# Four of 128 expert blocks multiply their tokens as 192 and 64 columns

## The chip, the cores and the metric
One core of a Trainium2 chip runs the whole program in one launch. The metric is the device time of that core in microseconds (us). Two runs of the kernel before took 1375.1 and 1375.38 us, median 1375.24.

## The reference
Two transformer blocks run one after the other on 256 tokens of 1024 features, in float32. The first ends in a retrieval feed-forward layer (PEER): each token chooses, for each of 8 heads, 16 of 16384 single-neuron experts by product keys, and the chosen experts are summed.

```
u_sel = peer_u[expert]
a = jax.nn.gelu(jnp.einsum('bqhkd,bqd->bqhk', u_sel, hb))
v_sel = peer_v[expert]
return jnp.einsum('bqhk,bqhkd->bqd', g * a, v_sel)
```

`g` is the softmax over the 16 chosen scores. The second block (two layers of window attention and gated mixing) follows; the change does not touch it.

## The kernel before
The kernel does not gather experts. It computes the gelu of all 16384 experts for all 256 tokens and multiplies it by a gate that is zero for those not chosen. The experts stand in 128 blocks of 128; a block is a weight tile of 128 partitions x 1024 (8 chunks of 128 features by 128 experts). The tokens `h2` stand transposed, 128 features by 8 chunks by 256 tokens.

Every such product is made in float32 accuracy from three products of rounded operands (type F32R, "round" below): a value is split into a rounded high part and the rest, and high x high, high x rest and rest x high are summed. The weight tile is split when it arrives: ScalarE rounds it into `wh` (line 229), VectorE subtracts to get `wl` (line 232). The tokens are split once, into `h2h` and `h2l`. The profile prints rounded operands of TensorE as f32; which matmuls are rounded is seen from the tiles: those on `wh`/`wl`, `zh`/`zl` and their like. Matmuls on plain F32 tiles, such as those of `proj_block` (line 463: 9 blocks of 8 matmuls, tile `wn` by `hf`) and the token sums (line 286: one column of ones by a 128x128 tile), are not.

The stage that matters here runs `for j in range(128)` over `u_block(j)`. A block loads `u[j]` by the SP queue (3 buffers), splits it (3 buffers each for `wh` and `wl`), and issues 24 matmuls into one PSUM tile of 128x256: for each chunk `k`, lines 246, 247 and 248 of `mm3`. Each matmul has a weight load (LDWEIGHTS) of its own. In the profile line 246 shows as `h2h,wh` (high by high), line 247 as `h2l,wh` and line 248 as `h2h,wl`. ScalarE then writes the gelu of the PSUM tile into `Z[:, j]` (line 927); while gates are built, the tokens whose gates are there already go through `at` and a multiplication on VectorE.

Between the blocks a generator of other steps is drawn on, by a budget of 1.45 per block against a cost that each step yields. First come the rest of the retrieval (top 16 of each head and decoding of the indices, on VectorE nearly alone, lines 822 to 884), then 64 gate steps: one-hot products on VectorE (lines 944 and following), 8 matmuls in f16 (line 951), and a multiplication of `Z` from PSUM. The order of instructions on each engine is the program's order. After the U stage, the V stage multiplies all of `Z` by the V blocks (line 1012), with 24 matmuls of 256 columns for each block, and the second transformer block follows.

The change touches `mm3` (lines 245 to 248), which all these products use, and `u_block`; `mm_block` (line 250) is what the blocks called before. The four changed blocks are j = 2, 34, 66 and 98. In the profiled execution, block 2 runs while VectorE does the retrieval, block 34 in the stretch between the retrieval and the gates, and blocks 66 and 98 among the gate steps.

Of the kernel before, what the change touches and what calls it, by code (L numbers as in the profile page):

```python
# [19 lines left out]
P = 128  # L20
T = 256
D = 1024
NCH = 8
# [141 lines left out]
def build(tc, d, out):  # L165
    nc = tc.nc
    ctx = ExitStack()
    V, S, G, TE = nc.vector, nc.scalar, nc.gpsimd, nc.tensor
# [42 lines left out]
    def nm(s):  # L211
        uid[0] += 1
        return f"{s}_{uid[0]}"
# [5 lines left out]
    def load(src):  # L219
        w = wpool.tile([P, 1024], F32, tag="w", name=nm("w"), bufs=WB)  # L220
        nc.sync.dma_start(w, src)
        return w

    def split(w, hi=S, lo=V, dst=None):
        if dst is None:
            dst = [wpool.tile([P, 1024], F32R, tag=t, name=nm(t), bufs=3) for t in ("wh", "wl")]
        wh, wl = dst
        if hi is S:
            S.activation(wh, w, AF.Copy)  # L229
        else:  # L230
            hi.tensor_copy(wh, w)
        lo.tensor_sub(wl, w, wh.bitcast(F32))  # L232
        return wh, wl
# [9 lines left out]
        return xh, xl  # L243

    def mm3(ps, sh, sl, mh, ml, first, last):
        TE.matmul(ps, sh, mh, start=first, stop=False)  # L246
        TE.matmul(ps, sh, ml, start=False, stop=False)  # L247
        return TE.matmul(ps, sl, mh, start=False, stop=last).ins  # L248

    def mm_block(ps, wh, wl, xh, xl, n=NCH, off=0, xoff=0):  # L250

        for k in range(n):
            sl = slice((off + k) * P, (off + k + 1) * P)
            i = mm3(ps, wh[:, sl], wl[:, sl], xh[:, xoff + k], xl[:, xoff + k], k == 0, k == n - 1)
        return i
# [8 lines left out]
    def mm_rows(src, idx, xh, xl, evac, each=None, sp=split, pre=(), **kw):  # L264

        ps = [psm.tile([P, 512], F32, tag="mm", name=nm("psr")) for _ in range(2)]
        for g in range(4):
            wh, wl = sp(pre[g] if g < len(pre) else load(src[idx + g]), **kw)
            for q in range(2):
                k = 2 * g + q  # L270
                for t in range(2):
                    ts_ = slice(t * P, (t + 1) * P)
                    mm3(ps[t], xh[:, k, ts_], xl[:, k, ts_],
                        wh[:, q * 512:(q + 1) * 512], wl[:, q * 512:(q + 1) * 512], k == 0, k == 7)
            if each:
                each()
        for t in range(2):
            evac(t, ps[t])

    def psum_mm():  # L280
        return psm.tile([P, 512], F32, tag="mm", name=nm("psmm"))
# [54 lines left out]
    def aux():  # L336
        return psa.tile([P, 512], F32, tag="aux", name=nm("aux"))
# [18 lines left out]
    for i in range(2):  # L356
        sl = slice(512 * i, 512 * i + 512)
        ps = aux()
# [20 lines left out]
    for i in range(4):  # L379
        ps = psum_mm()  # L380
# [21 lines left out]
    for k in range(NCH):  # L402
# [8 lines left out]
        sh = mod1[:, k, 1:2]  # L411
# [154 lines left out]
    for g in range(4):  # L566
        for q in range(2):
            k = 2 * g + q
# [16 lines left out]
    last = [None]  # L585
# [55 lines left out]
    for hp in range(4):  # L641
        ps = aux()
# [84 lines left out]
    for s in range(EARLY):  # L727
        w = nload()
        ps = psum_mm()
# [21 lines left out]
    h2h = pu.tile([P, NCH, T], F32R, name="h2h")  # L751
    h2l = pu.tile([P, NCH, T], F32R, name="h2l")
# [164 lines left out]
    last_mm, last_act = [None], [None]  # L917
    done = [0]

    def u_block(j):  # L920

        wh, wl = split(load(d["u"][j]))
        ps = psum_mm()
        last_mm[0] = mm_block(ps[:, :T], wh, wl, h2h, h2l)
        nd = done[0]
        if nd < T:
            last_act[0] = S.activation(Z[:, j, nd:], ps[:, nd:T], AF.Gelu_apprx_tanh).ins
        if nd:
            at = pr.tile([P, T], F32, tag="at", name=nm("at"), bufs=2)
            S.activation(at[:, :nd], ps[:, :nd], AF.Gelu_apprx_tanh)  # L930
            V.tensor_mul(Z[:, j, :nd], Z[:, j, :nd], at[:, :nd])
# [48 lines left out]
    for j in range(NJ):  # L980
        u_block(j)
        ju[0] = j + 1
        budget += STEP
        while budget > 0:
            c = next(todo, None)
            if c is None:
                break
            budget -= c
# [59 lines left out]
    def next2():  # L1048
        w = load(d["w2"][w2i[0]])
        w2i[0] += 1  # L1050
        return w

    def split2(w, dst=None):
        return split(w, dst=dst)
# [9 lines left out]
    def rows_tile(t, xh, xl, slabs, late_x=False):  # L1064

        ps = psum_mm()
        ts_ = slice(t * P, (t + 1) * P)
        for c in range(2):
            passes = [((xh, 0), (xh, 1)), ((xl, 0),)] if late_x else [((xh, 0), (xl, 0)), ((xh, 1),)]
            for r, ops in enumerate(passes):  # L1070
                for k in range(4 * c, 4 * c + 4):
                    sl = slice((k % 2) * 512, (k % 2) * 512 + 512)
                    for i, (x, part) in enumerate(ops):
                        last_mm[0] = TE.matmul(ps, x[:, k, ts_], slabs[k // 2][part][:, sl],  # L1074
                                               start=k == 0 and r == 0 and i == 0, stop=k == NCH - 1 and r == 1).ins
        return ps
# [15 lines left out]
    for l in range(2):  # L1092
        xh, xl = xh4, xl4
        if l == 0:
            first = []
# [30 lines left out]
        else:  # L1126
            ps = rows_tile(0, xh, xl, ahead, True)
# [11 lines left out]
        ps = aux()  # L1139
# [109 lines left out]
        for g in range(4):  # L1249
            ps = aux()  # L1250
# [8 lines left out]
        for b in range(4):  # L1259
            ps = aux()  # L1260
# [17 lines left out]
        mh = p4.tile([P, NCH, T], F32R, tag="mh", name=f"mh{l}")  # L1278
        ml = p4.tile([P, NCH, T], F32R, tag="ml", name=f"ml{l}")
        for n in range(NCH):  # L1280
            wh, wl = split2(next2())
# [16 lines left out]
        for t in range(2):  # L1298
            for hf in range(2):
                sl = slice(hf * 512, (hf + 1) * 512)  # L1300
# [14 lines left out]
        last = []  # L1315
# [48 lines left out]
```

## Time and profile before

| | |
|---|---|
| median of the runs | 1375.24 us |
| the profiled execution | 1375.99 us |
| its span, from the first to the last instruction | 1373.5 us |
| TensorE matmuls, busy | 1349.5 us (98%), 10472 |
| TensorE weight loads, busy | 1291.5 us (94%), 10472 |
| VectorE, busy | 1016.0 us (74%) |
| ScalarE, busy | 627.9 us (46%) |
| mean granted TensorE clock | 0.995 |

A matmul's duration in the profile runs from its start to the end of its drain, so consecutive matmuls overlap: what a matmul costs a full engine is the time from one start to the next. A row "x6" merges six instructions of the same form in a row: its duration runs from the first start to the last end. A weight load's row (PEld) overlaps the matmul before it.

### The profile page before, as it was taken

Reading aid. Unit: us, or ns where it says so; the run is one execution under the profiler, and the core shown is the slowest. Engines: PE = TensorE matmul, PEld = TensorE weight load, DVE = VectorE, ACT = ScalarE, POOL = GpSimd, SP = SyncE. Lnnn points to the kernel's source line nnn. Section 1 sums busy time; section 2 is a strip of 40 time slices with the busy share of each in tenths; the row PEclk is TensorE's granted clock in tenths of the full one; section 3 lists DMA queues with packets and bytes.
Section 4 is the critical chain, followed back from the end, with each engine's and each line's share of the span. In section 5 each row is a group of like instructions: output and inputs, shape, how many; then the busy total and the mean of one; then the engine's idle time right before and its main releaser. Section 6 shows DMA issues by size and latency. Waiting matters only on the chain.

```text
span 1373.5 us, 26275 instructions
## 1 busy us (share of the span) xinstructions
PE 1349.5 (98%) x10472; PEld 1291.5 (94%) x10472; DVE 1016.0 (74%) x2091; ACT 627.9 (46%) x1098; POOL 20.5 (1%) x35
## 2 busy tenths in 40 slices
PE   8999999999999999999999999999999999999997
PEld 6868899999999999999999999999999999799996
DVE  7898499974777777875777767666676867858676
ACT  5534255544544444444333333333345665356642
POOL 1000000000000000000000000000010000000000
PEclk9999999999999999999999999999999999999999
DMA  9886245566544454445666666656576466544663
GB/s 375 305 318 234 85 153 158 169 195 182 161 138 144 134 154 138 139 140 177 214 208 201 213 200 200 185 184 184 181 222 199 139 226 188 183 147 146 197 193 117
DMA packets 72554, 255.01 MB, mean 186 GB/s; under 512 B 8305, under 2 KB 10481, under 8 KB 72178
## 3 DMA queue, kind: packets, MB, share of 16 engines
q1 hardware_dynamic: 72434, 253.36, 57.7%
q8 instruction: 82, 1.34, 0.4%
q14 instruction: 38, 0.31, 0.1%
HBM read 252.28 MB, written 1.05 MB: 184 GB/s over the span
## 4 chain that ended last, share of the span: by engine, by line
PE 84%; DVE 11%; ACT 1%; DMA 1%; issue 1%; DVEq 0%; POOL 0%; SPq 0%; POOLq 0%; ACTq 0%
PE vacc L1012 26%; PE psmm L246 13%; PE psmm L248 13%; PE psmm L247 13%; PE aux L951 4%; DVE wl L232 3%; PE psmm L677 2%; PE psmm L1074 2%; PE aux L443 2%; PE psmm L463 1%; DMA w<-w 1%; PE iqp L443 1%; DVE Z L826 1%; DVE Z L824 1%; DVE Z L823 1%
## 5 line engine op out<-in xcount | busy, mean ns | idle before, releaser
L229 ACT ACTIVATE wh<-w 128x1024 fp32r<-128x1024 f32 x373 | 394.5, 1060 | 502.9 <-PE vacc L1012 206.8
L232 DVE TENSOR_TENSOR wl<-w,wh 128x1024 fp32r<-128x1024 f32 x373 | 455.2, 1221 | 157.3 <-ACT wh L229 155.0
L246 PE MATMUL psmm<-h2h,wh 128*128 128x256 f32 x1136 | 328.7, 289 | 0.0
L248 PE MATMUL psmm<-h2h,wl 128*128 128x256 f32 x1136 | 323.2, 285 | 3.6 <-DVE wl L232 3.5
L247 PE MATMUL psmm<-h2l,wh 128*128 128x256 f32 x1136 | 322.0, 283 | 0.0
L1012 PE MATMUL vacc<-zh,wh 128*128 128x256 f32 x1024 | 290.0, 284 | 0.4 <-DVE zh L241 0.4
L1012 PE MATMUL vacc<-zl,wh 128*128 128x256 f32 x1024 | 290.2, 284 | 0.0
L1012 PE MATMUL vacc<-zh,wl 128*128 128x256 f32 x1024 | 290.2, 284 | 0.0
L248 PEld LDWEIGHTS psmm<-h2h,wl 128*128 128x128 f32 x1136 | 217.5, 192 | 5.8 <-DVE wl L232 5.7
L246 PEld LDWEIGHTS psmm<-h2h,wh 128*128 128x128 f32 x1136 | 218.7, 193 | 0.1
L247 PEld LDWEIGHTS psmm<-h2l,wh 128*128 128x128 f32 x1136 | 218.1, 192 | 0.1
L1012 PEld LDWEIGHTS vacc<-zh,wh 128*128 128x128 f32 x1024 | 196.6, 192 | 0.5 <-issue 0.5
L1012 PEld LDWEIGHTS vacc<-zl,wh 128*128 128x128 f32 x1024 | 196.9, 192 | 0.0
L1012 PEld LDWEIGHTS vacc<-zh,wl 128*128 128x128 f32 x1024 | 196.9, 192 | 0.0
L246 PE MATMUL psmm<-xh,wh 128*128 128x256 f32 x544 | 154.4, 284 | 0.0
L248 PE MATMUL psmm<-xh,wl 128*128 128x256 f32 x544 | 152.2, 280 | 0.0
L247 PE MATMUL psmm<-xl,wh 128*128 128x256 f32 x544 | 151.9, 279 | 0.0
L246 PEld LDWEIGHTS psmm<-xh,wh 128*128 128x128 f32 x544 | 102.2, 188 | 0.9 <-ACT yh L1272 0.3
L248 PEld LDWEIGHTS psmm<-xh,wl 128*128 128x128 f32 x544 | 102.3, 188 | 0.7 <-DVE mx L1174 0.7
L247 PEld LDWEIGHTS psmm<-xl,wh 128*128 128x128 f32 x544 | 102.1, 188 | 0.1
L241 DVE CAST zh<-Z 128x256 fp32r<-128x256 f32 x128 | 37.4, 293 | 69.7 <-PE vacc L1012 69.3
L944 DVE TENSOR_TENSOR oh<-iohr,ij 128x1024 f16<-128x1024 f16 x64 | 44.2, 692 | 54.9 <-PE aux L951 54.9
(390 smaller groups left out, 1780.8 us busy)
## 6 DMA issues: line engine op xcount, KB each, us to landing
w<-u SPq DMA_DIRECT2D x128, 512.0 KB, 3.5
w<-v SPq DMA_DIRECT2D x128, 512.0 KB, 3.6
w<-w SPq DMA_DIRECT2D x122, 512.0 KB, 3.6
ada<-ada SPq DMA_DIRECT2D x40, 512.0 KB, 6.1
wn<-w SPq DMA_DIRECT2D x23, 512.0 KB, 5.4
w<-wa SPq DMA_DIRECT2D x8, 512.0 KB, 7.1
wb<-wb SPq DMA_DIRECT2D x8, 512.0 KB, 4.7
w<-ada SPq DMA_DIRECT2D x8, 512.0 KB, 3.5
```

The lines of the kernel that those rows point to most:

```text
L229: S.activation(wh, w, AF.Copy)
L232: lo.tensor_sub(wl, w, wh.bitcast(F32))
L241: hi.tensor_copy(xh, src)
L246: TE.matmul(ps, sh, mh, start=first, stop=False)
L247: TE.matmul(ps, sh, ml, start=False, stop=False)
L248: return TE.matmul(ps, sl, mh, start=False, stop=last).ins
L443: TE.matmul(ps, st, mv, start=first, stop=e and part == 1, skip_group_check=True)
L677: TE.matmul(ps, w[:, sl], y[:, k], start=half == 0 and q == 0 and k == 0, stop=half == 1 and k == 3, skip_group_check=True)
L944: V.tensor_tensor(oh, bc(iohr.unsqueeze(1), [P, 2, P, 4]), bc(ij16[:, :, k:k + 4].unsqueeze(2), [P, 2, P, 4]), ALU.is_equal)
L951: TE.matmul(o, oh[:, 0, :, q], ow[:, r, :, q], start=r == 0, stop=r == 1)
L1012: TE.matmul(acc[k // 2][:, k % 2], a[:, sl], b, start=(f and i == 0), stop=(l and i == 2), skip_group_check=True)
L1074: last_mm[0] = TE.matmul(ps, x[:, k, ts_], slabs[k // 2][part][:, sl], start=k == 0 and r == 0 and i == 0, stop=k == NCH - 1 and r == 1).ins
```

## The change
`u_block` takes its 256 tokens in two pieces for j = 2, 34, 66 and 98. For each chunk it first issues the three products for tokens 0 to 191, then the three for tokens 192 to 255, into the two parts of the same PSUM tile; only the very first matmul of the block carries the start flag. So such a block has 24 matmuls of 192 columns and 24 of 64, where it had 24 of 256. In `mm3` a flag is set that leaves out a check when the program is built.

```
 def mm3(ps, sh, sl, mh, ml, first, last):
-    TE.matmul(ps, sh, mh, start=first, stop=False)
-    TE.matmul(ps, sh, ml, start=False, stop=False)
-    return TE.matmul(ps, sl, mh, start=False, stop=last).ins
+    TE.matmul(ps, sh, mh, start=first, stop=False, skip_group_check=True)
+    TE.matmul(ps, sh, ml, start=False, stop=False, skip_group_check=True)
+    return TE.matmul(ps, sl, mh, start=False, stop=last, skip_group_check=True).ins
...
-    last_mm[0] = mm_block(ps[:, :T], wh, wl, h2h, h2l)
+    if j % 32 == 2:
+        for k in range(NCH):
+            sl = slice(k * P, (k + 1) * P)
+            for ts_ in (slice(0, 192), slice(192, T)):
+                last_mm[0] = mm3(ps[:, ts_], wh[:, sl], wl[:, sl], h2h[:, k, ts_], h2l[:, k, ts_], k == 0 and ts_.start == 0, k == NCH - 1)
+    else:
+        last_mm[0] = mm_block(ps[:, :T], wh, wl, h2h, h2l)
```

## Rows read from the trace of the kernel before
**Rows 1.** The page: busy us, share of the span and instructions of each engine.
```profile
PE 1349.5 (98%) x10472; PEld 1291.5 (94%) x10472; DVE 1016.0 (74%) x2091; ACT 627.9 (46%) x1098; POOL 20.5 (1%) x35
```
**Rows 2.** Chain of waits by time, 220 to 300 us: start, us, what.
```profile
224.76 1.12 DVE wl L232
...
279.96 1.15 DVE wl L232
281.15 0.38 PE psmm L248
```
**Rows 3.** Busy time by stretch: length; PE, PEld, DVE, ACT, POOL busy; PEclk; DMA.
```profile
225.50:229.00 3.50, 3.42 (x28) 3.10 (x26) 3.50 (x23) 1.33 (x2) 0.00 (x0) 1.00 0.43 150
...
284.00:360.00 76.00, 76.00 (x637) 76.00 (x636) 41.03 (x48) 38.44 (x57) 0.00 (x0) 1.00 0.62 189
360.00:626.00 266.00, 266.00 (x2226) 262.50 (x2224) 202.63 (x333) 119.71 (x278) 0.00 (x0) 1.00 0.46 143
...
656.00:1018.00 362.00, 361.64 (x3015) 361.46 (x3014) 253.62 (x403) 134.95 (x129) 0.13 (x1) 1.00 0.63 196
```
**Rows 4.** TensorE in order of time, first matmuls of blocks 34 and 35.
```profile
324.20 0.28 PE L246 MATMUL psmm<-h2h,wh 128*128 128x256 f32 x1
...
327.08 0.28 PE L246 MATMUL psmm<-h2h,wh 128*128 128x256 f32 x1
```
**Rows 5.** TensorE in order of time, a gate step and the start of block 66.
```profile
435.00 1.11 PE L951 MATMUL aux<-ow,oh 128*128 128x128 f16 x8
435.86 0.38 PE L246 MATMUL psmm<-h2h,wh 128*128 128x256 f32 x1
```
**Rows 6.** TensorE's waits from 284 us on: total us, times, longest us.
```profile
PE aux L1085 <- DVE xr L1335: 2.5, 1, 2.5
```
**Rows 7.** VectorE's waits from 284 to 660 us.
```profile
DVE oh L944 <- PE aux L951: 54.9, 62, 1.5
```
**Rows 8.** TensorE in order of time near the end, rounded, 512 columns.
```profile
1363.02 0.40 PE L1074 MATMUL psmm<-wlast_yh,ml 128*128 128x512 f32 x1
...
1364.42 0.40 PE L1074 MATMUL psmm<-wlast_yl,ml 128*128 128x512 f32 x1
```
**Rows 9.** Weight loads in order of time, token sums of one column.
```profile
119.90 0.97 PEld L286 LDWEIGHTS aux<-ones,nsq 128*128 128x128 f32 x8 [0.38 <-ACT nsq L654]
```
**Rows 10.** Line 463, unrounded: in order of time, then as a group.
```profile
84.26 1.46 PE L463 MATMUL psmm<-hf,wn 128*128 128x256 f32 x6
...
L463 PE MATMUL psmm<-hf,wn 128*128 128x256 f32 x144 | 33.9, 383 | 0.0
```
**Rows 11.** TensorE in order of time, second and third matmuls of blocks 3 to 6.
```profile
228.80 0.28 PE L247 MATMUL psmm<-h2l,wh 128*128 128x256 f32 x1
230.32 0.39 PE L248 MATMUL psmm<-h2h,wl 128*128 128x256 f32 x1 [1.24 <-DVE wl L232]
...
233.18 0.28 PE L247 MATMUL psmm<-h2l,wh 128*128 128x256 f32 x1
233.82 0.39 PE L248 MATMUL psmm<-h2h,wl 128*128 128x256 f32 x1 [0.36 <-DVE wl L232]
...
236.67 0.28 PE L247 MATMUL psmm<-h2l,wh 128*128 128x256 f32 x1
237.20 0.39 PE L248 MATMUL psmm<-h2h,wl 128*128 128x256 f32 x1 [0.24 <-DVE wl L232]
...
240.05 0.28 PE L247 MATMUL psmm<-h2l,wh 128*128 128x256 f32 x1
240.73 0.39 PE L248 MATMUL psmm<-h2h,wl 128*128 128x256 f32 x1 [0.40 <-DVE wl L232]
```
**Rows 12.** ScalarE in order of time: gelu of block 2, rounding for block 5.
```profile
233.30 0.36 ACT L927 ACTIVATE Z<-psmm 128x256 f32<-128x256 f32 x1
233.56 1.05 ACT L229 ACTIVATE wh<-w 128x1024 fp32r<-128x1024 f32 x1
```
**Rows 13.** VectorE in order of time, subtraction for block 5.
```profile
235.94 1.20 DVE L232 TENSOR_TENSOR wl<-w,wh 128x1024 fp32r<-128x1024 f32 x1
```

## The prediction
> **What bounds the kernel now.** I begin with the page's busy shares: TensorE is busy for 98% of the span, VectorE for 74% [rows 1]. So a longer U block should cost its whole extra length wherever TensorE leads, and the question is which of the four changed blocks (U2, U34, U66, U98) lie where it does not. The chain in order of time answers it for U2. From 224.76 us, where this part of it begins, to 281.15 us, where the chain goes over to a U matmul, its pieces are VectorE's [rows 2]: the retrieval, and between its steps the subtractions that give `wl`. U3's second matmul starts at 228.80 us [rows 11], so U2 is the 3 us before that, inside this stretch.
>
> The busy time by stretches says the same. From 225.5 to 229 us VectorE is busy for 3.50 of 3.50 us, from 284 to 360 us TensorE for 76.00 of 76.00, from 360 to 626 us for 266.00 of 266.00, and in the V stage for 361.64 of 362.00 [rows 3]. Since a matmul's row contains its drain, "busy" alone does not prove a dense engine; starts do. U34's first matmul starts at 324.20 us and U35's at 327.08 us, so 24 matmuls take 2.88 us, **0.120 us each** [rows 4]. In the gate stage, block and gate matmuls follow each other too: the eight of a gate start at 435.00 us and U66 at 435.86 us, 0.86 us [rows 5]. After 284 us TensorE has four waits to the end of the program, the longest 2.5 us for a transpose between the two layers [rows 6]; that one stands after work which starts later by the same amount, so it gives nothing back. VectorE in turn waits for the gate matmuls 62 times, 54.9 us in all [rows 7], so it has room and will not become the bound when TensorE is later. U34, U66 and U98 therefore pass their extra time to the end.
>
> **The change, part by part.** Nothing is moved and no tile, load, queue entry or semaphore wait is added: DMA, ScalarE and VectorE issue what they issued. The flag on the matmul helper changes a check at build time and costs nothing, there being no instruction for it. Each changed block gives up 24 matmuls of 256 columns and gets 24 of 192 and 24 of 64, each with its own weight load. That is 96 more matmuls and 96 more loads over the four blocks. The columns to stream stay 256 per chunk and product, so what is new is the price of the second instruction.
>
> No matmul of rounded (F32R) operands narrower than 256 columns is in the trace, so I bound the pair.
> - From below, by streaming alone. At 512 columns seven starts span 1363.02 to 1364.42 us, six steps of 0.233 us [rows 8]; with 0.120 at 256 [rows 4] that is a line of 0.007 + 0.00044 x columns. It gives 0.092 us for 192 and 0.035 us for 64, together 0.127 against 0.120: +0.17 us for a block.
> - From the rows with few columns. The one-column matmuls of the token sums have nothing to stream, and yet their eight weight loads of 128x128 take 0.97 us with the last one's 0.19 us included: (0.97 - 0.19) / 7 = **0.111 us each** [rows 9]. This is the time from one weight load to the next when the matmul hides none of it.
> - From above, by the price of unrounded fp32. Six records of 256 columns take 1.46 us, the last with its 0.38: 0.216 us each [rows 10], and the group counts 144 records for 9 blocks of 8 matmuls, two for each matmul. So 256 columns cost 0.432 us, 192 would cost 0.324, and 64 between 0.111 (one load) and 0.222 (two).
>
> I take the middle row. The 192-column matmul is nearest to the 256-column one, 0.120 us, for its stream of 0.092 is shorter than a weight load and cannot set the pace. The 64-column one is nearest to the one-column row, 0.111 us. A block then takes 24 x 0.231 = 5.54 us instead of 2.88, **+2.66 us**.
>
> Three blocks pay it in full: 3 x 2.66 = +8.0 us. U2's +2.66 us falls into waits for `wl`. U3's second and third matmul start at 228.80 and 230.32 us, where 0.12 would do: 1.40 us of room. U4 has 233.18 to 233.82 (0.52), U5 236.67 to 237.20 (0.41), U6 240.05 to 240.73 (0.56) [rows 11]. That is 2.89 us, so the delay is 1.26 us after U3, 0.74 after U4, 0.33 after U5 and nothing after U6, if VectorE is not late itself. What VectorE could wait for is ScalarE's rounding for U5, queued on ScalarE behind U2's gelu. That gelu starts at 233.30 us [rows 12], and U2 would end by 231.5 us, so nothing waits. If this cover failed, the sum would be 4 x 2.66 = 10.6 us.
>
> The profiled execution took 1375.99 us, of which 1373.5 is its span; with +8.0 it would take 1384.0. The median of the runs lies 0.75 lower, at 1375.24, which gives **1383.2 us**, +0.6%.
>
> **Rivals.**
> 1. *The weight load hides, and only columns count* (not slower). Place: all four blocks; price: the line above, +0.17 us each, three of them on the path: 1375.7 us. It decides if the next weights load twice as fast when the current matmul is short. Against it stands the 0.111 us of rows with one column [rows 9]; for it, only that those are unrounded operands. Chance 0.07. The Trainium skill, in "TensorE: Matmul & The Clock Gate", section "Back-to-back issue gap", gives a warm isolated matmul N/2.4 + 2.5 ns: 82.5 and 29.2 ns here, less than the one of 256, and so a result some 0.6 us under the time before. By that section's sustained figure, 131 ns for 512 columns with its load, this trace disagrees, with 233 ns.
> 2. *Narrow rounded matmuls lose their single pass* (slower). Place: the array; price: the unrounded rate, 24 x (0.324 + 0.111 - 0.120) = +7.6 us for a block, up to 24 x (0.324 + 0.222 - 0.120) = +10.2. It decides if the single pass is only to be had from 256 columns up. For it: unrounded fp32 does take four times as long for its columns, and every rounded matmul that I see here has 256 columns or more, so the trace cannot exclude it. Against it: nothing in the trace changes rate with width alone; 512 and 256 columns lie near one line through zero. U2 would then end at 236.4 us, its gelu would start 3.1 us late, the rounding behind it would end near 237.9 us and VectorE's subtraction, now at 235.94 us [rows 13], would slip by 2.0 us: 3 x 7.6 + 2.0 = +24.8 us, **1400.0 us**; at the upper price 3 x 10.2 + 4.6 = +35 us, 1410 us. Chance 0.20.
> 3. *U2 is not covered*: 1385.9 us. The row of ScalarE's gelu speaks against it [rows 12]. It lies inside the forecast's range and takes 0.05 of its 0.70.
>
> **How the numbers follow.** The forecast with its bounds on either side (both pieces at 0.111: 1382.6; both at 0.120 and U2 uncovered: 1386.8) has 0.70, rival 2 has 0.20, rival 1 0.07, something that I do not see 0.03, of which 0.01 is a gain. The range starts at 1380, under the forecast's lowest sum, and leaves out rival 1; it ends at 1402, with the cheaper half of rival 2, which makes 0.70 + 0.11 = 0.81. Slower by over 2% means over 1402.7 us, which is about what a measurement of this kernel can tell from no change: the dearer part of rival 2, 0.09, and 0.01 unseen. Faster by over 2%: 0.01. Within: 0.89.
>
> **What would show it.** After the change, U34 should have 48 matmuls that start 0.11 to 0.12 us apart, whichever their width, and the next block should start 5.5 us after it; equal steps for both widths are the mark of the weight load. Steps of 0.09 and 0.035 us would be rival 1, and 0.32 for the wide piece rival 2. U3's wait for `wl` should be gone and U7 should start when it does now. The gates should keep 0.86 us and VectorE's waits for them should grow by about a block's 2.7 us, once at U66 and once at U98. The V stage should have the same length and start 8 us later. I am wrong if the steps of the two widths differ much, or if the shift at 284 us is not near zero.

## The result and the profile after

The changed kernel takes 1390.93 us (median of 2 runs) against 1375.24: the ratio is 1.0118, with a 95% interval of 1.0094 to 1.0142. I had forecast 1383.2 us, +8.0; it is +15.7. The time lies inside the range I gave, but the change cost twice what I worked out, and half of that came by a mechanism that I had not seen. The profiled execution took 1390.69 us with a span of 1388.1.

The page of the changed kernel has 96 matmuls more, as counted, and VectorE's and ScalarE's work is the same.

```profile
PE 1358.9 (98%) x10568; PEld 1303.2 (94%) x10568; DVE 1016.7 (73%) x2091; ACT 628.9 (45%) x1098; POOL 20.6 (1%) x35
```

Block 34 first, where nothing disturbs it: TensorE in order of time, changed kernel.

```profile
332.83 0.25 PE L246 MATMUL psmm<-h2h,wh 128*128 128x192 f32 x1
...
333.15 0.21 PE L246 MATMUL psmm<-h2h,wh 128*128 128x64 f32 x1
333.20 0.28 PE L247 MATMUL psmm<-h2l,wh 128*128 128x64 f32 x1
333.31 0.28 PE L248 MATMUL psmm<-h2h,wl 128*128 128x64 f32 x1
333.42 0.34 PE L246 MATMUL psmm<-h2h,wh 128*128 128x192 f32 x1
333.59 0.27 PE L247 MATMUL psmm<-h2l,wh 128*128 128x192 f32 x1
...
338.11 0.36 PE L246 MATMUL psmm<-h2h,wh 128*128 128x256 f32 x1
```

The block takes 338.11 - 332.83 = 5.28 us for 48 matmuls, where 24 took 2.88 [rows 4]. The starts of the matmuls are uneven (the next one follows 0.05 us behind the first 64-column matmul of a chunk and 0.17 behind the first 192-column one), so the pace is better read from the weight loads of the same stretch:

```profile
333.06 0.19 PEld L246 LDWEIGHTS psmm<-h2h,wh 128*128 128x128 f32 x1
333.17 0.19 PEld L247 LDWEIGHTS psmm<-h2l,wh 128*128 128x128 f32 x1
333.28 0.19 PEld L248 LDWEIGHTS psmm<-h2h,wl 128*128 128x128 f32 x1
333.39 0.19 PEld L246 LDWEIGHTS psmm<-h2h,wh 128*128 128x128 f32 x1
333.50 0.19 PEld L247 LDWEIGHTS psmm<-h2l,wh 128*128 128x128 f32 x1
333.62 0.19 PEld L248 LDWEIGHTS psmm<-h2h,wl 128*128 128x128 f32 x1
333.73 0.19 PEld L246 LDWEIGHTS psmm<-h2h,wh 128*128 128x128 f32 x1
```

Six steps from load to load in 0.67 us: 0.112 us each, whether the matmul behind has 192 or 64 columns. That is the price read before from the one-column matmuls [rows 9]. It is read as the pace of the loads and not of the matmuls, since one matmul here starts 0.05 us behind another (333.15 and 333.20).

Now block 2. Here are the second to fourth matmuls of block 5 in the changed kernel, where before the third started 0.53 us after the second [rows 11]:

```profile
237.21 0.28 PE L247 MATMUL psmm<-h2l,wh 128*128 128x256 f32 x1
246.90 0.58 PE L248 MATMUL psmm<-h2h,wl 128*128 128x256 f32 x1 [9.41 <-DVE wl L232]
247.28 0.42 PE L246 MATMUL psmm<-h2h,wh 128*128 128x256 f32 x1
247.49 0.41 PE L247 MATMUL psmm<-h2l,wh 128*128 128x256 f32 x1
```

TensorE waits 9.41 us for block 5's `wl`, and then its matmuls start 0.213 us apart instead of 0.120. What the `wl` waited for is seen from ScalarE and VectorE, changed kernel, each in order of time: two of ScalarE's retrieval copies and its rounding for block 5, then VectorE's subtraction with its neighbours.

```profile
231.56 3.71 ACT L852 ACTIVATE Z<-Z 128x2048 f16<-128x2048 f32 x2 [3.96 <-DVE Z L849]
235.18 1.04 ACT L229 ACTIVATE wh<-w 128x1024 fp32r<-128x1024 f32 x1
```
```profile
244.48 1.23 DVE L879 TENSOR_TENSOR Z<-io16r,Z 128x2048 f16<-128x2048 f16 x1
245.62 1.23 DVE L232 TENSOR_TENSOR wl<-w,wh 128x1024 fp32r<-128x1024 f32 x1
246.75 0.30 DVE L875 TENSOR_TENSOR Z<-Z 128x128 f16<-128x128 f32 x1
```

The rounding is done at 236.2 us. The subtraction starts at 245.62 us, where it started at 235.94 [rows 13]. So for 9.4 us it waited for nothing but its turn: retrieval steps stand ahead of it that stood behind it before. The busy time by stretches of the changed kernel (columns as in [rows 3]) shows what came of it:

```profile
237.00:246.00 9.00, 0.49 (x5) 0.29 (x3) 9.00 (x59) 0.71 (x2) 0.00 (x0) 0.81 0.00 0
246.00:252.00 6.00, 5.10 (x24) 5.10 (x25) 6.00 (x15) 3.29 (x4) 0.00 (x0) 0.50 0.56 162
252.00:284.00 32.00, 32.00 (x266) 32.00 (x266) 31.62 (x94) 16.27 (x23) 0.00 (x0) 0.99 0.58 170
```

VectorE is busy for all 9.00 us of the first stretch, with TensorE at 0.49. TensorE's granted clock is 0.50 in the second stretch, 1.2 of 2.4 GHz, after a stretch in which it did almost nothing. The Trainium skill, in "TensorE: Matmul & The Clock Gate", part 1, says that the clock is halved when TensorE has been idle and restored by activity; this trace agrees, with 0.213 against 0.120 us per matmul. In the third stretch TensorE no longer waits: `wl` now comes early, and the waits of before, up to block 19, are gone.

The bill up to the end of the U stage, by the starts of blocks in both traces: +11.83 us at block 6. Of these, 0.54 are how late block 5 started (block 2 had started 0.51 late already, so its own extra length was used up by then), 9.16 the longer wait (9.69 us between the second and the third matmul, against 0.53), and 2.1 the half clock. The waits that fell away behind it give 3.2 back, which leaves +8.63 at block 20. Blocks 34, 66 and 98 add 2.40, 2.40 and 2.41, and the blocks right behind 34 and 66 another 0.08 and 0.07. The sum is +15.99 where the V stage begins (656.73 us before, 672.72 after), and the same where it ends. At the end of the span it is 14.7. The 1.3 us between the two need not come from the change: what follows the V stage took 347.9 us in the profiled execution before, 346.6 in this one, and between 345.1 and 347.8 in those of the eight experiments, with the same instructions. For differences of a few us the start of the V stage is therefore the better measure, and it stands beside the times below.

### The profile page after: what moved, and what is told of

The parts are those of the page before. It is cut to its first block, busy times and chain, and to the rows that moved or that the text cites. A ratio compares the mean times of both kernels' runs of the same rounds, so it can differ in the third digit from the quotient of the medians.

```text
span 1388.1 us, 26467 instructions
## 1 busy us (share of the span) xinstructions
PE 1358.9 (98%) x10568; PEld 1303.2 (94%) x10568; DVE 1016.7 (73%) x2091; ACT 628.9 (45%) x1098; POOL 20.6 (1%) x35
## 4 chain that ended last, share of the span: by engine, by line
PE 88%; DVE 8%; ACT 1%; issue 1%; DMA 1%; DVEq 0%; POOL 0%; SPq 0%; POOLq 0%
PE vacc L1018 26%; PE psmm L246 15%; PE psmm L248 14%; PE psmm L247 14%; PE aux L957 4%; PE psmm L677 2%; PE psmm L1080 2%; DVE wl L232 2%; PE aux L443 2%; PE psmm L463 1%; PE iqp L443 1%; PE psr L248 1%; DVE Z L826 1%; PE psr L246 1%; PE psr L247 1%
## 5 line engine op out<-in xcount | busy, mean ns | idle before, releaser
L248 PE MATMUL psmm<-h2h,wl 128*128 128x256 f32 (+1 forms) x1168 | 331.1, 283 | 9.4 <-DVE wl L232 9.4
L246 PE MATMUL psmm<-h2h,wh 128*128 128x256 f32 (+1 forms) x1168 | 337.9, 289 | 0.0
L247 PE MATMUL psmm<-h2l,wh 128*128 128x256 f32 (+1 forms) x1168 | 331.2, 284 | 0.0
L248 PEld LDWEIGHTS psmm<-h2h,wl 128*128 128x128 f32 x1168 | 224.4, 192 | 9.6 <-DVE wl L232 9.6
L246 PEld LDWEIGHTS psmm<-h2h,wh 128*128 128x128 f32 x1168 | 225.5, 193 | 0.1
L247 PEld LDWEIGHTS psmm<-h2l,wh 128*128 128x128 f32 x1168 | 224.8, 193 | 0.1
```

The lines of the kernel that those rows point to most:

```text
L246: TE.matmul(ps, sh, mh, start=first, stop=False, skip_group_check=True)
L247: TE.matmul(ps, sh, ml, start=False, stop=False, skip_group_check=True)
L248: return TE.matmul(ps, sl, mh, start=False, stop=last, skip_group_check=True).ins
```

## The experiments

The theory: each split block costs 2.4 us, because its matmuls go at the pace of their weight loads, and block 2's go into waits as forecast, but the planner that orders the instructions when the program is built set VectorE's and ScalarE's differently because of block 2, and that order costs +8.6 us. The main rivals: a split block costs 3.9 us wherever it lies; or the longer block 2 itself holds up VectorE through the buffers. The time of the kernel before was 1375.21 us in the first four runs and 1375.47 in the last four.

**Blocks 34, 66 and 98 alone.**
```
-        if j % 32 == 2:
+        if j in (34, 66, 98):
```


> Blocks 34, 66 and 98 are split, block 2 is whole; VectorE and ScalarE have the order of instructions of the kernel before. Theory (each split block costs its weight loads, +2.4 us, and block 2 costs the rest of the +15.7 us by the changed order of VectorE): +7.3 us, about 1382.5 us. Rival (a split block costs a quarter of the whole, 3.9 us, wherever it lies): +11.8 us, about 1387 us.

Measured: 1382.04 us, ratio 1.0058 (1.0044 to 1.0071), +6.8 us. In its trace the V stage starts 7.65 us later than before, 0.30 of it from ahead of block 34. The rival's 11.8 is out.

**Block 2 alone.**
```
-        if j % 32 == 2:
+        if j == 2:
```


> Block 2 alone is split; VectorE and ScalarE have the order of the changed kernel. Theory: the subtraction for block 5 comes about 9.7 us later on VectorE, TensorE waits once for some 9 us, its clock falls, and +8.6 us are left where the retrieval ends: about 1383.9 us. Rival (a quarter of the whole): +3.9 us, 1379 us. First forecast (covered): 1375 us.

Measured: 1383.54 us, ratio 1.0064 (1.0050 to 1.0078), +8.3 us. In its trace the V stage starts 8.25 us later. Block 2 costs as much as the three others together (the intervals overlap), and the two parts add up to the whole: 0.58% + 0.64% against 1.18%. My forecast for block 2, nothing, is refuted as the change was made. From 200 to 330 us VectorE and ScalarE have in this trace the order of the changed kernel, record for record; with blocks 34, 66 and 98 alone split, they have that of the kernel before.

**All four blocks split, order of before.** VectorE's and ScalarE's instructions around blocks 5 to 20 (141 and 27 of them) are chained in the order of the kernel before. The edges fix the order of issue and add no semaphore.
```
+    def hold(engine, order):
+        seq = [i for i in nc.cur_bb.bb.instructions if i.engine == engine]
+        for a, b in zip(order, order[1:]):
+            tc.add_manual_dep(seq[b], seq[a].name, mybir.DependencyInfo(
+                mybir.DependencyClass.NoSync, mybir.DependencyReason.DATA), reason="issue_after")
+    hold(mybir.EngineType.DVE, [
...
+    ])
+    hold(mybir.EngineType.Activation, [
...
+    ])
```


> All four blocks are split as in the changed kernel, but VectorE and ScalarE are held to the order of instructions of the kernel before, by edges that order the issue and add no wait. Theory (the order is what block 2 costs, its own +2.4 us fall into waits for wl): +7.3 us, about 1382.5 us, block 20 of the U stage no later than before. Rival (the longer block 2 itself delays VectorE or ScalarE through the buffers): +15.7 us, 1391 us.

Measured: 1382.44 us, ratio 1.0057 (1.0043 to 1.0071), +7.2 us; the V stage starts 7.80 us later. Here the first forecast's mechanism can be watched. TensorE in order of time in this run, second and third matmuls of blocks 3 to 6:

```profile
231.73 0.28 PE L247 MATMUL psmm<-h2l,wh 128*128 128x256 f32 x1
231.84 0.28 PE L248 MATMUL psmm<-h2h,wl 128*128 128x256 f32 x1
...
234.61 0.28 PE L247 MATMUL psmm<-h2l,wh 128*128 128x256 f32 x1
234.73 0.28 PE L248 MATMUL psmm<-h2h,wl 128*128 128x256 f32 x1
...
237.48 0.28 PE L247 MATMUL psmm<-h2l,wh 128*128 128x256 f32 x1
237.62 0.38 PE L248 MATMUL psmm<-h2h,wl 128*128 128x256 f32 x1
...
240.48 0.28 PE L247 MATMUL psmm<-h2l,wh 128*128 128x256 f32 x1
241.15 0.39 PE L248 MATMUL psmm<-h2h,wl 128*128 128x256 f32 x1 [0.40 <-DVE wl L232]
```

The waits of blocks 3, 4 and 5 [rows 11] are used up by the longer block 2, and block 6 waits 0.40 us again as it did before. This run is 0.40 us late from block 0 on; block 6's third matmul is 0.42 us late, so block 2's extra time has gone. The same matmuls, weight loads and buffers as in the changed kernel cost 8.5 us less with another order: the rival by which block 2's length delays VectorE is out.

**No block split, order of the changed kernel.** The same helper on the kernel before, with the other order.

> No block is split; VectorE and ScalarE are held to the order of instructions of the changed kernel. Theory: the order alone costs what block 2 cost: TensorE waits some 11 us for the subtraction for block 5, its clock falls to the lower level as after the change, +8.6 us, about 1383.9 us. Rival (a split block is needed for the loss): 1375 us.

Measured: 1383.47 us, ratio 1.0062 (1.0049 to 1.0076), +8.3 us, as much as splitting block 2 alone; the V stage starts 8.03 us later. The longest wait for `wl` is 8.9 us, where I expected some 11. Its stretches, columns as before:

```profile
237.00:246.00 9.00, 0.50 (x2) 0.30 (x2) 9.00 (x57) 0.59 (x2) 0.00 (x0) 0.77 0.00 0
246.00:252.00 6.00, 5.22 (x24) 5.22 (x25) 6.00 (x15) 3.42 (x4) 0.00 (x0) 0.50 0.55 171
```

The empty stretch and the half clock are there without a narrow matmul in the kernel. The order alone does it.

**Block 2 twice at 256 columns.** The edit is against the kernel before.
```
-        last_mm[0] = mm_block(ps[:, :T], wh, wl, h2h, h2l)
+        if j == 2:
+            for k in range(NCH):
+                sl = slice(k * P, (k + 1) * P)
+                for o in (0, T):
+                    last_mm[0] = mm3(ps[:, o:o + T], wh[:, sl], wl[:, sl], h2h[:, k], h2l[:, k], k == 0 and o == 0, k == NCH - 1)
+        else:
+            last_mm[0] = mm_block(ps[:, :T], wh, wl, h2h, h2l)
```


> Block 2 alone is changed: each of its 24 matmuls of 256 columns is issued twice, the second time into the unused half of its PSUM tile, so it takes 2.88 us more on TensorE, more than the split's 2.4. The planner knows the length of such matmuls and moves the subtraction for block 5 by 17 places on VectorE, where the split moved it by 46. Theory (the planner takes the split block for much longer than it is): a wait of some 2 to 3 us at block 5, clock kept, +1 to +3 us at the end of the retrieval: about 1376 to 1378 us. Rival (any longer block 2 leads to the late order and its loss): +8 us or more, 1383 us.

Measured: 1376.92 us, ratio 1.0018 (1.0009 to 1.0027), +1.4 us; the V stage starts 2.58 us later. TensorE's waits for `wl` from 200 us on (total us, times, longest us), kernel before, then this run:

```profile
PE psmm L248 <- DVE wl L232: 3.5, 8, 1.2
```
```profile
PE psmm L248 <- DVE wl L232: 4.1, 4, 2.6
```

One wait is longer than any before, and still short. From block 2's start to block 3's this run takes 6.01 us (225.50 to 231.51), the run with block 2 alone split 5.65 (225.84 to 231.49). So block 2 is the longer one here, and yet costs about a sixth by the times and a third by the starts of the V stage (2.58 against 8.25 us). Neither the length of the block nor the number of its matmuls (48 in both) is then enough for the late order. On VectorE the subtraction for block 5 stands 17 places later than before in this run, and 46 places later with the split.

**Subtractions ahead of the retrieval's steps**, whole blocks. The edit is against the kernel before.
```
-        lo.tensor_sub(wl, w, wh.bitcast(F32))
+        last_wl[0] = lo.tensor_sub(wl, w, wh.bitcast(F32)).ins
...
-            c = next(todo, None)
+            with tc.issue_after(last_wl[0]) if j < 44 else nullcontext():
+                c = next(todo, None)
```


> No block is split; the retrieval's VectorE steps that are traced after block j (j under 44) are held behind block j's subtraction, so that the planner can't move them ahead of it. Theory (in the kernel before, TensorE waits some 7 us in all between blocks 0 and 20 for subtractions that stand behind retrieval steps; the steps have time until block 44): those waits go, -6 to -8 us, about 1368 us. Rival (the retrieval ends later and the gates with it, what is gained is given back behind it): 1375 us or above.

Measured: 1369.43 us, ratio 0.9962 (0.9949 to 0.9976), -6.0 us: faster than both kernels, by little but clear of the noise. The V stage starts 5.57 us earlier. TensorE's waits for `wl` are gone from the list, and it is busy in all of the stretch that held them; VectorE now works on the retrieval beyond 284 us, 58.95 us of the second stretch against 41.03 before [rows 3]:

```profile
200.00:284.00 84.00, 84.00 (x701) 83.76 (x700) 75.58 (x261) 43.99 (x68) 0.00 (x0) 1.00 0.59 181
284.00:360.00 76.00, 75.94 (x633) 75.65 (x632) 58.95 (x143) 41.42 (x60) 0.00 (x0) 1.00 0.56 176
```

**The same with the four blocks split.**

> The four blocks are split as in the changed kernel, with the same holding of the retrieval's VectorE steps behind the subtractions. Theory (no waits are left to hide block 2, and the order can't be upset): the time of the whole kernel with this order plus 4 x 2.4 = 9.7 us, about 1377 to 1378 us, 13 us under the changed kernel. Rival (the planner's order is upset elsewhere): over 1385 us.

Measured: 1379.42 us, ratio 1.0032 (1.0020 to 1.0044); the V stage starts 4.88 us later than in the kernel before. The time is 1.4 us above the 1377 to 1378 expected, mostly because the order itself gave 1369.43 and not 1368. Against the run before it, it is +10.0 us for four blocks, where 9.7 was expected. By the starts of blocks in the two traces, block 2 adds 2.47 us up to block 4, like the others: there are no waits for it to fall into. Another 0.8 us come in between blocks 20 and 33, which no experiment followed up.

**128 and 128 columns** in blocks 34, 66 and 98. The edit is against the first experiment.
```
-                for ts_ in (slice(0, 192), slice(192, T)):
+                for ts_ in (slice(0, 128), slice(128, T)):
```


> Blocks 34, 66 and 98 are split into 128 and 128 columns instead of 192 and 64; order as in the kernel before. Theory (a narrow matmul costs its weight load, 0.112 us, whatever its width): +7.3 us, as with 192 and 64, about 1382.3 us. Rival (columns set part of the price): the steps of the 128-column matmuls are under 0.10 us or over 0.13 us, +3 us or +11 us and more.

Measured: 1382.94 us, ratio 1.0056 (1.0042 to 1.0069), +7.5 us; the V stage starts 7.93 us later, 0.52 of it from ahead of block 34. The weight loads of block 34 are as far apart as with 192 and 64:

```profile
325.06 0.19 PEld L247 LDWEIGHTS psmm<-h2l,wh 128*128 128x128 f32 x1
...
325.95 0.19 PEld L246 LDWEIGHTS psmm<-h2h,wh 128*128 128x128 f32 x1
```

Eight steps in 0.89 us, 0.111 each. At 64, 128 and 192 columns the loads set the price and the width does not.

## Why the prediction was wrong

- **The price of a narrow matmul: right.** I had 0.231 us for a pair, it is 0.112 x 2 = 0.224. For a block that is 24 x (0.224 - 0.120) = 2.50 us and not 2.66; the starts of blocks show 2.40, and behind blocks 34 and 66 the 0.08 and 0.07 more. My 0.120 for the 192-column piece, taken from its nearest row, was the poorer choice; the row of one column held for both. The Trainium skill gives columns / 1.2 ns for a weight load in "TensorE: Matmul & The Clock Gate", section "LDWEIGHTS (loading the stationary operand)", 107 ns for 128 columns; the trace has 112 from one load to the next.
- **Three blocks in full: right.** +7.4 us in the trace from block 34 up to the V stage (15.99 - 8.63), +6.8 us by the run of these three alone; the forecast was +8.0.
- **Rivals 1 and 2: refuted.** Hidden loads would have given steps of 0.035 us for the narrow piece, a lost single pass 0.32 for the wide one; the loads go on at 0.112 behind both. Two figures beside them were off. The "0.6 us under the time before" sets 82.5 + 29.2 ns from the formula quoted there against the 120 ns of the trace; by the formula alone 256 columns take 109.2 ns, and no gain follows. And unrounded fp32 takes 3.6 times as long here (0.432 against 0.120 us), not four.
- **"Nothing is moved": wrong, and this is the step that failed.** On it rests the term of the sum that puts block 2 at nothing, "if VectorE is not late itself". I wrote that DMA, ScalarE and VectorE "issue what they issued". They issue the same instructions, but VectorE and ScalarE in another order. My introduction says that the order on each engine is the program's order; that is false as well. A planner sets it when the program is built, and a change of matmuls on TensorE can move VectorE's work, as the two orders show. The trace of before could have told: the order of the program has all of one token half's index decoding ahead of the other half's, while on VectorE the second half's conversion (line 849) stands ahead of the first half's decoding (line 865). VectorE in order of time, kernel before:

```profile
244.36 0.27 DVE L849 CAST Z<-Z 128x256 f32<-128x256 uint32 x1
...
246.45 0.21 DVE L865 CAST Z<-Z 128x128 f32<-128x128 uint32 x1
```

- **Block 2 covered: right as a mechanism, wrong for this kernel.** With the order held, its time goes into the waits of blocks 3 to 5, as worked out from [rows 11]. With the planner's order block 2 costs +8.6 us at block 20. I had named as danger that ScalarE's rounding for block 5 comes late behind block 2's gelu. It starts 1.6 us later than before (235.18 against 233.56 [rows 12]), but for another reason: ScalarE's order changed too, and both retrieval copies now stand ahead of it. It ends 0.3 us after the old start of the subtraction; the other 9.4 us are VectorE's order.
- **The marks.** Block 7 should have started when it did; it started at 255.07 us instead of 243.47. I had said that a shift other than zero at 284 us would prove me wrong: it is +8.6.
- **The range: luck.** That 1390.93 us lies between 1380 and 1402 is owed to rival 2, for which alone the range reached so far up, and which did not happen. The order of the engines was not among the rivals; it belongs to the 0.03 for what I did not see.

Open: why the planner delayed the subtraction. That it takes narrow rounded matmuls for much dearer than they are on the chip fits the two orders (46 places against 17, for less time), but no run shows it: the runs show what the order does, not how it was reckoned.

## What to carry to other kernels

Where a framework orders the instructions when the program is built, compare the order on every engine after any edit, also on engines that the edit does not touch; edges that hold the order tell its cost from the edit's own. Where each matmul loads its own stationary operand, as here, the loads set a floor for narrow matmuls, which is to be read from the narrowest matmuls in the trace. Work with slack that stands ahead of work on which the bound engine waits is worth holding back: here that gave 6 us, without any change to the arithmetic. And where a part of the kernel that the edit does not touch varies by 2 to 3 us between executions, effects of that size are better read from a point ahead of it in the traces.

## What was not expected of the hardware

The wait of 9.4 us cost more than itself: TensorE came back at half clock, and 25 steps from 247.28 us on took 0.213 us instead of 0.120, 2.3 us in all. After a wait of 2.6 us in the same place the clock stayed, as the stretch of the run with block 2 twice at 256 columns shows:

```profile
237.00:246.00 9.00, 6.32 (x51) 5.91 (x50) 9.00 (x50) 3.12 (x6) 0.00 (x0) 1.00 0.30 101
```

And the starts of matmuls behind narrow ones are uneven, 0.05 and 0.17 us, while the weight loads tick evenly at 0.112.
